# Hybrid layer on one core: which engine builds the S5 stage's block-diagonal pieces, diagonal terms and weight splits

## Chip, core and metric

The kernel runs on one core of a Trainium2 chip. TensorE does the matrix products, VectorE, ScalarE and GpSimd the elementwise work, and SyncE's queue issues nearly all transfers. In the rows they are PE (and PEld for its weight loads), DVE, ACT, POOL and SP. The metric is the device time of one execution in microseconds (us), lower is better; a comparison goes by the median of several runs.

## The reference, cut to what matters

One decoder layer on 1024 tokens of width 1024: RMSNorm, one combined projection, three branches (an S5 diagonal complex state-space model, a Mamba-2 SSD, cross-attention into 256 memory tokens), a gated merge, an output projection, then a gated convolutional MLP and a last norm. All data are float32. The part around the change is the S5 branch:

```python
bbr = fr[..., None] * b_re - fi[..., None] * b_im
bbi = fr[..., None] * b_im + fi[..., None] * b_re
bu_re = jnp.einsum('blgk,gpk->blgp', ug, bbr)
bu_im = jnp.einsum('blgk,gpk->blgp', ug, bbi)
...
_, _, xr, xi = lax.associative_scan(combine, (a_re, a_im, bu_re, bu_im), axis=1)
y = jnp.einsum('gkp,blgp->blgk', c_re, xr) - jnp.einsum('gkp,blgp->blgk', c_im, xi)
return y.reshape(bsz, L, D_S5) + d * u
```

There are 64 groups of 16 channels with 64 states each.

## The kernel before, in words

Each float32 product is made of three matmuls on halves: a weight tile `wr` comes from memory, ScalarE rounds it into `wh`, and the low part `wl = wr - wh` is a subtraction on a second engine (`split_into`, L140). `w_ent` (L260) makes these splits for the jobs to come; the set `on_pool` (L226) names the jobs whose subtraction is on GpSimd instead of VectorE. A ring of six `wh`/`wl` pairs runs ahead of TensorE, and three `wr` tiles ahead of that: the next load of a `wr` tile waits in SyncE's queue, which is served in order, until the last reader of the old one, the subtraction, is done.

The stage of the change lies about 523 to 780 us into the span. TensorE projects the four query tiles (`qt`) and nine gate tiles (`gt`), in half tiles called `gh`, with 24 matmuls each; after every 12 of them a step of the S5 work (`s5_work`, L773) may be put in, paced by `RATE_S5` and `S5_LAG`. S5 runs in four rounds (q = 0 to 3, 16 groups each), and a round goes like this:

- `b_maps` (L825): six VectorE operations make the tiles `s5BAr`, `s5BAi`; eight columns of them are copied (the imaginary part negated) into the block-diagonal tile `s5bd`, in four pieces of 64 partitions x 128 elements.
- `phases` and `double` (L888, L896): GpSimd builds the rotation tiles `s5Rr`, `s5Ri` in seven doublings, 42 small operations, from 8 up to 512 elements per partition; `s5ph` is their scratch.
- `b_transpose` and `c_maps`: TensorE transposes (`s5bps`, `s5cps`), ScalarE copies, and VectorE makes the maps `s5CAr`, `s5CAi` in six operations of 1024 elements, the last two of them with both inputs in SBUF.
- `lag_maps` (L865): TensorE multiplies `s5CAr`, `s5CAi` with `s5bd` (16 pairs of matmuls, `s5kps`); ScalarE copies the result to a tile (`s5w` in the rows), a diagonal term `s5dg` is made and added to it, and the tile goes over memory (`kS`) into the tile `s5T`.
- `sums`, `scan`, `back`: TensorE makes `s5sr`, `s5si`; VectorE rotates them with `s5Rr`, `s5Ri`, scans, and rotates back into `s5Hr`, `s5Hi`, in two halves.
- `outputs` and `gelu`: TensorE makes `s5yp` of the round before; ScalarE and VectorE make `s5Y`, which is stored (`yS`) from a single buffer.

While this stage is written down, TensorE, ScalarE and SyncE keep the order of the program (`TE.on = SY.on = S.on`, L1151); VectorE's and GpSimd's order is set by a scheduler. Each engine then runs its own list strictly in order, and waits at the head of it. All operations go through one recording helper, so every row says L51; rows are told apart by tile names.

Of the kernel before, what the change touches and what calls it, by code (L numbers as in the profile page):

```python
# [12 lines left out]
ALU = mybir.AluOpType  # L13
# [4 lines left out]
P = 128  # L18
# [8 lines left out]
C_U, C_Z, C_X, C_DT, C_Q, C_G = 0, 1024, 3072, 6144, 6176, 6688  # L27
# [31 lines left out]
def hybrid_layer(ctx: ExitStack, tc: tile.TileContext, a: dict, out: bass.AP):  # L59
    nc = tc.nc  # L60
    V, S, G, TE, SY = (InOrder(tc, e) for e in (nc.vector, nc.scalar, nc.gpsimd, nc.tensor, nc.sync))
# [63 lines left out]
    def tt(o, i0, i1, op, e=V):  # L125
        e.tensor_tensor(out=o, in0=i0, in1=i1, op=op)

    def ts(o, i0, s1, op0, s2=None, op1=None, e=V):
        if s2 is None:
            e.tensor_scalar(out=o, in0=i0, scalar1=s1, scalar2=None, op0=op0)  # L130
        else:
            e.tensor_scalar(out=o, in0=i0, scalar1=s1, scalar2=s2, op0=op0, op1=op1)
# [4 lines left out]
    def copy(o, i, scale=1.0):  # L137
        S.activation(out=o, in_=i, func=AF.Copy, scale=scale)
# [9 lines left out]
    def bc(ap, n):  # L148
        return ap.unsqueeze(len(ap.shape)).to_broadcast(list(ap.shape) + [n])
# [41 lines left out]
    G_S5, G_ATT, G_SSD = range(0, 9), range(9, 12), range(12, 24)  # L191

    def win(c0, m=P):
        return ("p", "w_in", 0, KD, c0, m)
# [28 lines left out]
    T_AT = {n: i for i, n in enumerate(("T1", "T2", "T3", "T4"))}  # L223
    dents = [(p, k) for p in PRODS for k in range(NK)]

    on_pool = {win(C_U), win(C_U + P)} | {win(C_Q + m * P) for m in range(4)} | {win(C_G + m * P) for m in G_S5}  # L226
    raw_list, ents = [], []
    for n, jb in enumerate(jobs):
        if jb[0] == "w":
# [543 lines left out]
    def s5_work():  # L773

        with ExitStack() as es:
# [4 lines left out]
            bd = sp.tile([P, 2, NCH, 2, 16], F32, name="s5bd")  # L780
# [8 lines left out]
            def wt():  # L789
                return sp.tile([P, 8, P], F32, tag="w", name="s5w", bufs=2)  # L790

            def fl(t, s0, n):
                return t.rearrange("p j s k -> p j (s k)")[:, :, s0 * 16:(s0 + n) * 16]
# [17 lines left out]
            def cmap(o, s0, wr, wi, p2, jj):  # L811

                shp = [P, 8, 8, 16]
                orr, oi = (t[:, :, s0:s0 + 8, :] for t in o)
                w = [x.unsqueeze(2).to_broadcast(shp) for x in (wr, wi)]
                p_ = [bc(x[:, jj, :], 16) for x in p2]
                t1, t2 = (wt().rearrange("p j (t k) -> p j t k", t=8) for _ in range(2))
                tt(orr, w[0], p_[0], ALU.mult)
                tt(t1, w[1], p_[1], ALU.mult)
                tt(oi, w[0], p_[1], ALU.mult)  # L820
                tt(t2, w[1], p_[0], ALU.mult)
                tt(orr, orr, t1, ALU.subtract)
                tt(oi, oi, t2, ALU.add)

            def b_maps(jj, braw):  # L825

                BAr = sp.tile([P, 8, 8, 16], F32, tag="BAr", name="s5BAr")
                BAi = sp.tile([P, 8, 8, 16], F32, tag="BAi", name="s5BAi")
                cmap((BAr, BAi), 0, braw[:, 0], braw[:, 1], (pfr, pfi), jj)
                for g2 in range(2):  # L830
                    pp = slice(g2 * 64, (g2 + 1) * 64)
                    G.tensor_copy(bd[pp, 0, :, g2, :], BAr[pp, :, 7, :])
                    G.tensor_scalar(out=bd[pp, 1, :, g2, :], in0=BAi[pp, :, 7, :], scalar1=-1.0,
                                    scalar2=0.0, op0=ALU.mult, op1=ALU.add)
                return BAr, BAi

            def c_transpose(craw):
# [27 lines left out]
            def lag_maps(q, CA):  # L865

                ksq = kS[q % 2]
                ktw = wt()
                for hh in range(2):
                    kps = ps.tile([32, 4, P], F32, tag="s", name="s5kps")  # L870
                    for j in range(4):
                        jx = hh * 4 + j
                        for ri in range(2):
                            TE.matmul(kps[:, j, :], bd[:, ri, jx].rearrange("p g k -> p (g k)"),
                                      fl(CA[ri], 0, 8)[:, jx, :], start=ri == 0, stop=ri == 1)
                    KT = ktw[0:32, 4 * hh:4 * hh + 4, :]
                    copy(KT, kps)
                    dg = sp.tile([32, 4, 16], F32, tag="dg", name="s5dg")
                    tt(dg, bc(dk[:, 8 * q + 4 * hh:8 * q + 4 * hh + 4], 16),
                       id16.unsqueeze(1).to_broadcast([32, 4, 16]), ALU.mult, G)  # L880
                    tt(KT[:, :, 0:16], KT[:, :, 0:16], dg, ALU.add, G)
                    SY.dma_start(out=ksq[4 * hh:4 * hh + 4].rearrange("j p x -> p j x"), in_=KT)
                kv_ = ksq.rearrange("j (g k) x -> k j g x", g=2)
                for s in range(8):
                    tz = Tz[s * 16:(s + 1) * 16].rearrange("p (j g) t k -> p j g (t k)", g=2)
                    SY.dma_start(out=tz[:, :, :, s * 16:P], in_=kv_[:, :, :, 0:P - s * 16])
# [114 lines left out]
            for q in range(5):  # L1001
# [4 lines left out]
                if q < 4:  # L1006
                    U, braw, craw = nl
                    BA = b_maps(jj, braw)
                    R = phases(jj)
                    double(R, jj, range(5))  # L1010
# [16 lines left out]
                if q == 4:  # L1027
                    s5_end.append(lambda: y_store(qo, 1, Y1))
                    break
                lag_maps(q, CA)  # L1030
                if old:
                    y_store(qo, 1, Y1)
# [16 lines left out]
    id16 = cp.tile([32, 16], F32, name="id16")  # L1049
# [814 lines left out]
```

## Time and profile before

| what | us |
|---|---|
| median of 3 runs | 2323.52 (2322.17 to 2324.78) |
| profiled execution | 2324.85 |
| its span, first to last instruction | 2323.1 |
| TensorE matmul busy | 2210.0 (95%) |
| VectorE busy | 1649.3 (71%) |
| ScalarE busy | 981.4 (42%) |
| GpSimd busy | 857.6 (37%) |
| TensorE busy in 543 to 563, 614 to 625, 672 to 683, 735 to 755 | 6.15 of 20, 5.73 of 11, 6.40 of 11, 15.32 of 20 |

TensorE is the engine whose list is never far from being the limit, so the places where it stands still are what counts. The page's slices show a 3 to 6 tenths busier GpSimd and a less busy TensorE in the 9th to 12th of 40 slices, which is the S5 stage. The table's last line holds the four stretches of that stage where TensorE does little.

### The profile page before, as it was taken

Reading aid. Unit: us, or ns where it says so; the run is one execution under the profiler, and the core shown is the slowest. Engines: PE = TensorE matmul, PEld = TensorE weight load, DVE = VectorE, ACT = ScalarE, POOL = GpSimd, SP = SyncE. Lnnn points to the kernel's source line nnn. Section 1 sums busy time; section 2 is a strip of 40 time slices with the busy share of each in tenths; the row PEclk is TensorE's granted clock in tenths of the full one; section 3 lists DMA queues with packets and bytes.
Section 4 is the critical chain, followed back from the end, with each engine's and each line's share of the span. In section 5 each row is a group of like instructions: output and inputs, shape, how many; then the busy total and the mean of one; then the engine's idle time right before and its main releaser. Section 6 shows DMA issues by size and latency. Waiting matters only on the chain. (4 is left out here: it accounts for less than half of the span.)

```text
span 2323.1 us, 31155 instructions
## 1 busy us (share of the span) xinstructions
PE 2210.0 (95%) x11239; PEld 1828.8 (79%) x11239; DVE 1649.3 (71%) x2310; ACT 981.4 (42%) x1746; POOL 857.6 (37%) x689
## 2 busy tenths in 40 slices
PE   6989999997898999999989999999999999999997
PEld 5777888886777788777768878889878888888886
DVE  7899878876664685989564455642888888886665
ACT  4444554552222266566342121222345545545543
POOL 4423333337666003888337522220123343320111
PEclk9999999998999999999999999999999999999999
DMA  4323434455353446898777764523323323229654
GB/s 149 110 82 91 127 109 127 127 139 96 92 107 82 128 139 231 272 315 268 232 258 240 226 207 145 163 73 119 109 68 96 118 86 118 86 102 330 223 186 152
DMA packets 380474, 356.06 MB, mean 153 GB/s; under 512 B 35616, under 2 KB 323232, under 8 KB 380320
## 3 DMA queue, kind: packets, MB, share of 16 engines
q1 hardware_dynamic: 379168, 349.89, 48.5%
q10 hardware_dynamic: 1152, 4.19, 0.4%
q8 instruction: 88, 1.44, 0.3%
q14 instruction: 66, 0.54, 0.1%
HBM read 255.97 MB, written 98.04 MB: 152 GB/s over the span
## 5 line engine op out<-in xcount | busy, mean ns | idle before, releaser
L51 DVE TENSOR_TENSOR wl<-wr,wh 128x512 fp32r<-128x512 f32 (+1 forms) x275 | 233.4, 859 | 168.6 <-ACT wh L51 167.0
L51 ACT ACTIVATE wh<-wr 128x512 fp32r<-128x512 f32 (+1 forms) x305 | 185.9, 625 | 326.7 <-PE g L51 149.1
L51 PE MATMUL g<-hlH,wh 128*128 128x512 f32 x736 | 288.6, 394 | 11.3 <-ACT hlH L51 5.7
L51 PE MATMUL g<-hlL,wh 128*128 128x512 f32 x736 | 290.1, 394 | 4.6 <-DVE hlL L51 4.5
L51 PE MATMUL g<-hlH,wl 128*128 128x512 f32 x736 | 288.1, 392 | 0.0
L51 POOL TENSOR_TENSOR wS<-wr 128x512 f32<-128x512 f32 x82 | 132.0, 1610 | 374.4 <-DMA wr<-in_w_up 181.9
L51 PE MATMUL gh<-hlH,wh 128*128 128x512 f32 (+1 forms) x464 | 191.9, 414 | 0.0
L51 PE MATMUL gh<-hlH,wl 128*128 128x512 f32 (+1 forms) x464 | 181.6, 391 | 0.0
L51 PE MATMUL gh<-hlL,wh 128*128 128x512 f32 (+1 forms) x464 | 181.5, 391 | 0.0
L51 PEld LDWEIGHTS g<-hlH,wh 128*128 128x128 f32 x736 | 139.2, 189 | 42.4 <-issue 6.8
L51 PEld LDWEIGHTS g<-hlL,wh 128*128 128x128 f32 x736 | 139.0, 189 | 37.9 <-DVE hlL L51 9.9
L51 ACT ACTIVATE wh<-wS 128x512 fp32r<-128x512 f32 x164 | 102.2, 628 | 145.0 <-PE wA L51 89.1
L51 PEld LDWEIGHTS g<-hlH,wl 128*128 128x128 f32 x736 | 139.2, 189 | 28.4
L51 DVE TENSOR_TENSOR wl<-wS,wh 128x512 fp32r<-128x512 f32 x164 | 135.5, 831 | 36.6 <-ACT wh L51 36.4
L51 POOL TENSOR_TENSOR wS<-wr,wS 128x512 f32<-128x512 f32 x41 | 95.1, 2318 | 109.0 <-DVE wl L51 99.1
L51 PE MATMUL dP<-wl,ah 128*128 128x512 f32 x308 | 120.0, 390 | 0.2 <-DVE wl L51 0.2
L51 PE MATMUL dP<-wh,ah 128*128 128x512 f32 x308 | 119.9, 389 | 0.1
L51 PE MATMUL dP<-wh,al 128*128 128x512 f32 x308 | 119.8, 389 | 0.0
L51 POOL TENSOR_TENSOR x1f<-x1f,gfin 128x512 f32<-128x512 f32 x16 | 23.0, 1459 | 224.3 <-ACT sq L51 224.3
L51 PEld LDWEIGHTS gh<-hlH,wh 128*128 128x128 f32 (+1 forms) x464 | 86.2, 186 | 24.1 <-issue 5.7
L51 DVE TENSOR_TENSOR al<-ra,ah 128x512 fp32r<-128x512 f32 x77 | 56.3, 731 | 66.9 <-ACT ah L51 66.8
L51 PEld LDWEIGHTS gh<-hlL,wh 128*128 128x128 f32 (+1 forms) x464 | 86.3, 186 | 21.6 <-issue 3.6
(383 smaller groups left out, 6004.4 us busy)
## 6 DMA issues: line engine op xcount, KB each, us to landing
wr<-in_w_in SPq DMA_DIRECT2D x76, 512.0 KB, 3.7
wr<-in_w_up SPq DMA_DIRECT2D x44, 512.0 KB, 3.7
xc<-xcS SPq DMA_DIRECT2D x32, 640.0 KB, 5.8
ra<-aS SPq DMA_DIRECT2D x77, 256.0 KB, 5.2
seg<-aD SPq DMA_DIRECT2D x32, 512.0 KB, 6.5
gi<-gS SPq DMA_DIRECT2D x32, 512.0 KB, 5.4
xcS<-xv SPq DMA_DIRECT2D x24, 512.0 KB
gS<-gt SPq DMA_DIRECT2D x24, 512.0 KB, 3.0
```

The costliest lines, as they stand in the source:

```text
L51: r = f(*args, **kw)
```

## The change

Three sets of elementwise operations go from GpSimd to VectorE; the arithmetic is the same.

```diff
-    on_pool = {win(C_U), win(C_U + P)} | {win(C_Q + m * P) for m in range(4)} | {win(C_G + m * P) for m in G_S5}
+    on_pool = {win(C_U), win(C_U + P)}
...
-                    G.tensor_copy(bd[pp, 0, :, g2, :], BAr[pp, :, 7, :])
-                    G.tensor_scalar(out=bd[pp, 1, :, g2, :], in0=BAi[pp, :, 7, :], scalar1=-1.0,
-                                    scalar2=0.0, op0=ALU.mult, op1=ALU.add)
+                    V.tensor_copy(bd[pp, 0, :, g2, :], BAr[pp, :, 7, :])
+                    ts(bd[pp, 1, :, g2, :], BAi[pp, :, 7, :], -1.0, ALU.mult)
...
                     tt(dg, bc(dk[:, 8 * q + 4 * hh:8 * q + 4 * hh + 4], 16),
-                       id16.unsqueeze(1).to_broadcast([32, 4, 16]), ALU.mult, G)
-                    tt(KT[:, :, 0:16], KT[:, :, 0:16], dg, ALU.add, G)
+                       id16.unsqueeze(1).to_broadcast([32, 4, 16]), ALU.mult)
+                    tt(KT[:, :, 0:16], KT[:, :, 0:16], dg, ALU.add)
```

The first line concerns 13 jobs of two entries, so 26 subtractions `wl`; the second 16 pieces of `s5bd`; the third 8 terms `s5dg` and 8 additions. The lists of TensorE, ScalarE and SyncE are the same as before. GpSimd's and VectorE's lists change.

GpSimd at the end of the first round, before: the last operation of the phases, then all that followed it.

```order
L51 TENSOR_TENSOR s5Ri<-s5Ri,s5ph 128x8x64
L51 TENSOR_TENSOR wl<-wr,wh 128x512
L51 COPY s5bd<-s5BAr 64x8x16 x2
L51 TENSOR_SCALAR s5bd<-s5BAi 64x8x16 x2
L51 TENSOR_TENSOR wl<-wr,wh 128x512 x2
L51 TENSOR_TENSOR s5w<-s5w,s5dg 32x4x16
L51 TENSOR_TENSOR s5dg<-s5dk,id_389 32x64
L51 TENSOR_TENSOR s5w<-s5w,s5dg 32x4x16
L51 TENSOR_TENSOR s5dg<-s5dk,id_389 32x64
L51 MEMSET s5D_4769 128x8
```

In the changed list the phases are followed by a memset of the decay tile and at once by the phases of the next round; the pieces of `s5bd`, which stood behind all 42 operations, are gone from the list.

VectorE in the second round, a piece of the difference: the end of `b_maps`, then the operations of `gelu` and the first of `c_maps`.

```order
 L51 TENSOR_TENSOR s5BAr<-s5BAr,s5w 128x1024
 L51 TENSOR_TENSOR s5BAi<-s5BAi,s5w 128x1024
+L51 COPY s5bd<-s5BAr 64x8x16
+L51 TENSOR_SCALAR s5bd<-s5BAi 64x8x16
+L51 COPY s5bd<-s5BAr 64x8x16
+L51 TENSOR_SCALAR s5bd<-s5BAi 64x8x16
+L51 TENSOR_TENSOR wl<-wr,wh 128x512 x2
 L51 SCALAR_TENSOR_TENSOR s5Y<-s5Y,s5yp 128x4x128 x4
 L51 TENSOR_TENSOR s5CAr<-s5cps,s5pwr 128x8x128
```

The four pieces of `s5bd` now come right behind the maps that they are copied from, ahead of `gelu` and of `c_maps`, and a pair of `wl` with them.

VectorE later in the same round, between the two halves of `scan` and `back`: another pair of `wl` stands between the second scan and the second `back`.

```order
 L51 TENSOR_TENSOR s5w<-s5w 128x512 x2
 L51 SCALAR_TENSOR_TENSOR s5W<-s5D_5271,s5w 128x512 x2
+L51 TENSOR_TENSOR wl<-wr,wh 128x512 x2
 L51 TENSOR_TENSOR s5Hr<-s5W,s5Rr 128x4x127
 L51 TENSOR_TENSOR s5w<-s5W,s5Ri 128x4x127
```

`back` now has to wait for these subtractions, and they for ScalarE's `wh`. In the first round the pair stands between the first scan and the first `back`.

## Rows read from the trace of the kernel before

**Rows 1.** Who waited for whom, 500 to 770 us: total us, times, longest.

```profile
POOL wl L51 <- ACT wh L51: 63.8, 7, 19.5
...
PE s5kps L51 <- POOL s5bd L51: 31.0, 7, 13.7
DVE s5CAr L51 <- ACT s5CAi L51: 30.8, 4, 10.2
...
ACT s5Y L51 <- DMA yS<-s5Y: 19.3, 2, 16.5
```

**Rows 2.** TensorE in order of time: start, us, operation [idle before, released by].

```profile
556.92 0.63 PE L51 MATMUL s5kps<-s5CAr,s5bd 128*32 128x128 f32 x2 [13.75 <-POOL s5bd L51]
557.66 0.64 PE L51 MATMUL s5kps<-s5CAi,s5bd 128*32 128x128 f32 x2
...
562.27 0.38 PE L51 MATMUL s5kps<-s5CAr,s5bd 128*32 128x128 f32 x2
562.49 0.38 PE L51 MATMUL s5kps<-s5CAi,s5bd 128*32 128x128 f32 x2
...
619.90 0.64 PE L51 MATMUL s5kps<-s5CAi,s5bd 128*32 128x128 f32 x2 [2.46 <-POOL s5bd L51]
...
677.24 0.63 PE L51 MATMUL s5kps<-s5CAi,s5bd 128*32 128x128 f32 x2 [1.35 <-POOL s5bd L51]
...
736.04 0.64 PE L51 MATMUL s5kps<-s5CAi,s5bd 128*32 128x128 f32 x2 [2.43 <-POOL s5bd L51]
...
740.74 1.09 PE L51 MATMUL s5sr<-s5U,s5BTr 128*64 128x128 f32 x16
...
746.34 1.97 PE L51 MATMUL s5sr<-s5U,s5BTr 128*64 128x128 f32 x16 [3.63 <-DVE s5Y L51]
```

**Rows 3.** Busy time in a stretch: PE, PEld, DVE, ACT, POOL, granted clock, DMA.

```profile
543.00:563.00 20.00, 6.15 (x34) 4.71 (x34) 3.33 (x3) 0.68 (x2) 17.08 (x21) 0.66 0.26 73
```

**Rows 4.** SyncE's queue, its longest wait: total us, times, longest.

```profile
SPq L51 <- POOL s5D L51: 25.6, 1, 25.6
```

**Rows 5.** SyncE's queue in order of time: the store behind that wait.

```profile
737.82 3.92 SPq L51 DMA_DIRECT2D yS<-s5Y  x8
```

**Rows 6.** VectorE in order of time: the last map of each round.

```profile
544.70 1.63 DVE L51 TENSOR_TENSOR s5CAi<-s5CAi,s5w 128x1024 f32<-128x1024 f32 x1
...
613.98 2.28 DVE L51 TENSOR_TENSOR s5CAi<-s5CAi,s5w 128x1024 f32<-128x1024 f32 x1
...
672.64 2.06 DVE L51 TENSOR_TENSOR s5CAi<-s5CAi,s5w 128x1024 f32<-128x1024 f32 x1
...
732.92 1.31 DVE L51 TENSOR_TENSOR s5CAi<-s5CAi,s5w 128x1024 f32<-128x1024 f32 x1
```

**Rows 7.** Groups by shape, 500 to 770 us: count | busy us, mean ns | idle before.

```profile
L51 POOL TENSOR_TENSOR wl<-wr,wh 128x512 fp32r<-128x512 f32 x26 | 37.0, 1438 | 67.3 <-ACT wh L51 63.8 <-issue 1.9 <-POOL s5bd L51 0.8
```

**Rows 8.** Groups by shape, VectorE: one split in this stretch, and small scalings.

```profile
L51 DVE TENSOR_TENSOR wl<-wr,wh 128x512 fp32r<-128x512 f32 x1 | 0.7, 686 | 0.0
...
L51 DVE TENSOR_SCALAR dgi<-ident,ivt 128x128 f32<-128x128 f32 x8 | 1.9, 280 | 0.0
```

**Rows 9.** First round in order of time: a scan, ScalarE's splits, the last back, outputs.

```profile
570.81 2.33 DVE L51 TENSOR_TENSOR_SCAN s5W<-s5D,s5w 128x512 f32<-128x512 f32 x2
...
572.93 1.14 ACT L51 ACTIVATE wh<-wr 128x512 fp32r<-128x512 f32 x2
...
578.23 0.68 DVE L51 SCALAR_TENSOR_TENSOR s5Hi<-s5Hi,s5w 128x508 f32<-128x508 f32 x1
...
583.12 0.60 PE L51 MATMUL s5yp<-s5U,s5T 128*128 128x128 f32 x4
```

**Rows 10.** Second round in order of time: GpSimd's phases, first and last, TensorE's sums.

```profile
586.79 8.42 POOL L51 TENSOR_TENSOR s5ph<-s5keep,s5Ri 128x8 f32<-128x8 f32 x1
...
617.95 1.27 POOL L51 TENSOR_TENSOR s5Ri<-s5Ri,s5ph 128x512 f32<-128x512 f32 x1
...
624.65 1.09 PE L51 MATMUL s5sr<-s5U,s5BTr 128*64 128x128 f32 x16
```

## The prediction, made before the changed kernel ran

> **What bounds the kernel now.** I read the share of busy time first (TensorE 95%), then, for the S5 stage, the waits by engine, TensorE's own list in order of time, SyncE's queue, and last VectorE's list at each place where TensorE stands still. The waits of the stage [rows 1] are long on nearly every engine, and most cost nothing: GpSimd is idle 63.8 us for ScalarE's `wh`, VectorE 30.8 us for ScalarE's copies. The line to pick out is the one whose waiting engine is TensorE: `s5kps` waits 31.0 us in seven waits for GpSimd's `s5bd`, the longest 13.7. TensorE's list shows where: at 556.92, and in the other rounds just ahead of the rows at 619.90, 677.24 and 736.04 [rows 2]. These are the pieces that the GpSimd list of the section on the change puts behind all phases. The stretch around the first wait has TensorE busy 6.15 of 20 us and GpSimd 17.08 [rows 3]: one engine stands for the other.
>
> A smaller stall is TensorE's 3.63 us at 746.34, named after VectorE's `s5Y` [rows 2]. Followed back it is a chain of buffers: SyncE's queue stands 25.6 us [rows 4] behind a load whose `wr` GpSimd has not read yet, the store `yS` comes out only at 737.82 and takes 3.92 [rows 5], ScalarE waits 16.5 us for it before it may write the single `s5Y` again [rows 1], VectorE waits for ScalarE and TensorE for VectorE. Behind the stall the same 16 matmuls take 1.97 instead of 1.09 us [rows 2].
>
> So in this stage TensorE loses 31.0 + 3.6 us in plain sight, and some more to the clock: the granted clock is 0.66 in that first stretch [rows 3], the lower level of 1.2 GHz for part of it. The 16 pairs of `s5kps` start over 5.57 us (556.92 to 562.49); at the distance of the last two, 0.22, fifteen gaps would take 3.3, so 2.3 us go there [rows 2].
>
> **The change, part by part.** The sum is made against the profiled execution, 2324.85 (span 2323.1 and 1.75 around it), which lies 1.33 above the median of 2323.52. The gain is then taken off the median.
>
> *Pieces of `s5bd`.* On VectorE they stand right behind `b_maps`, ahead of `c_maps`. So they are done before `s5CAr` and `s5CAi`, the other operands of the same matmuls, and `s5CAi` becomes the last one. Its last operation ends at 544.70 + 1.63 = 546.33, 613.98 + 2.28 = 616.26, 672.64 + 2.06 = 674.70 and 732.92 + 1.31 = 734.23 [rows 6]. In the first round one more `wl` ahead of the maps makes it 546.33 + 0.69 = 547.0. Against the starts of the second half of the operands in rows 2 (the first matmul with `s5CAi`) this is a gain of 557.66 - 547.0 = 10.6, 619.90 - 616.26 = 3.6, 677.24 - 674.70 = 2.5 and 736.04 - 734.23 = 1.8: together 18.5 of the 31.0. The remaining 12.5, about 3 a round, stay as a wait for VectorE.
>
> *What VectorE pays for it.* The 26 subtractions cost GpSimd 1438 ns each, 37.0 us in all [rows 7]. VectorE does one of the same shape in 686 ns, so 17.8 us come to it; and a small scaling of 128 x 128 took 280 ns [rows 8], which I take for each of the pieces (64 x 128) and as an upper end for the diagonal terms: 32 operations, at most 9 us. Per round that is four pieces, 1.1, a pair of `wl` ahead of `c_maps`, 1.4, and another pair by the scans. Ahead of `c_maps` VectorE waits for ScalarE 30.8 us in four waits [rows 1], the copies of TensorE's transposes; that wait hides 2.5 us except where it is itself shorter, and without this cover the round would gain 2.5 less (four rounds: 10). The diagonal terms lie behind `s5kps`, where VectorE waits for TensorE's sums, and cost nothing.
>
> *The pair by the scans.* It waits for `wh`, and everything behind it on VectorE's list (`back`, then `s5Hr`, `s5Hi` for TensorE's outputs) waits too. In the first round the first scans end at 570.81 + 2.33 = 573.14 and `wh` is there at 572.93 + 1.14 = 574.07: with the second subtraction 574.07 + 0.69 = 574.76, a delay of 1.6. The last operation of `back` ends at 578.23 + 0.68 = 578.91, the outputs start at 583.12: 4.2 us of slack [rows 9] cover it. If that cover were gone, it would cost 1.6 a round.
>
> *GpSimd.* In the second round its phases end at 617.95 + 1.27 = 619.2, with splits and pieces in between; the sums, whose rotation is the first reader, start at 624.65 [rows 10]. It has some 5 us of slack and loses work, so nothing new is late there.
>
> *A lock between the two engines.* At 586.79 an operation on 8 elements took GpSimd 8.42 us, where one on 512 elements took 1.27 [rows 10]; VectorE was in `b_maps` at the time. So a long VectorE stretch can hold a GpSimd operation up, and the subtractions add to such stretches. The price here lies between nothing, since the phases have about 5 us in hand, and 2.5 a round when it is VectorE's last two maps that wait for a GpSimd operation of 1.27 each. I take nothing: the maps ran beside the phases before as well, and their stretched times (2.28 and 2.06 against 1.31) are in my sum.
>
> The Trainium skill speaks against the change at this place ("SBUF — State Buffer", section "Who interferes with whom"): a VectorE instruction with two inputs in SBUF contends with a GpSimd instruction that reads SBUF, and whichever issues second is blocked until the other is done. `wl` has two such inputs. The 8.42 us agree with it. By that rule at its worst the time is that of the second rival below; by the rows' slack it changes nothing.
>
> *The store chain.* Without `wl` on GpSimd SyncE's queue does not stand behind the phases; `yS` leaves earlier, `s5Y` is free, and the stall of 3.63 goes. The sixteen matmuls behind it, twice (`s5sr` and `s5si`), run at 1.09 instead of 1.97: 1.8 more. Together 5.4; the bound below is nothing, if VectorE's `wl` hold the queue as long.
>
> Sum: 18.5 + 5.4 = 23.9. 2324.85 - 23.9 = 2300.95 for an execution like the profiled one, 2299.6 against the median.
>
> **Rivals.**
> - *More is gained.* If the shorter stalls no longer bring the clock down, up to 2.3 us a round come back; I take 2.3 for the first and half for each other, 5.8. If the last maps also run unstretched, at 1.31 each [rows 6] (1.0 + 0.75 + 0.3 = 2.0 for `s5CAi`, as much for its sister `s5CAr`), 4.0 more: 2299.6 - 9.8 = 2289.8. Against it: stalls of 2.46 and 1.35 were enough for matmuls of 0.63 to 0.64 in the rows [rows 2].
> - *The lock takes part of it.* Each of the last two maps waits for one GpSimd operation more, 2 x 1.27 = 2.5 a round, 10.2 in four: 2309.8. The same time comes out if ScalarE's copies don't cover the added 2.5. For it: 8.42 [rows 10]; against it: GpSimd has less to do.
> - *Slower: VectorE waits where GpSimd waited.* GpSimd was idle 63.8 us for `wh`, 44.3 without the longest wait [rows 1], some 11.1 a round. If these waits fall to VectorE ahead of `back`, each round pays 11.1 less the 4.2 of slack [rows 9], 27.6 in all, and 4 x 1.4 for the subtractions: 2299.6 + 33.2 = 2332.8. It decides once the delay passes 4.2 + 23.9 / 4 = 10.2 a round. Against it: in the first round ScalarE's `wh` come 0.9 after the scans [rows 9], not 11 us.
> - *It does not do what it says.* The stalls move to a later place where TensorE waits for a transfer or for VectorE: 2323.5.
>
> **How the numbers follow.** Forecast 2299.6, chance 0.53; its own range is 2294 (the clock comes back) to 2305 (the store chain stays, +5.4). More gained 0.17, the lock 0.20, slower 0.05, nothing 0.05. The range takes the first three and 2 us around the outer ones: 2288 to 2312. A measurement of this kernel tells about 0.2%, 4.6 us, from no change: faster 0.90, same 0.05, slower 0.05.
>
> **What would show it.** Right: TensorE's `s5kps` waits some 3 us a round for VectorE's `s5CAi` and no more for `s5bd`; SyncE's queue has no wait of 25 us for GpSimd; ScalarE's wait of 16.5 for `yS` and TensorE's of 3.63 at `s5sr` are gone; GpSimd ends its phases before the sums. Wrong: a wait for `wh` on VectorE of more than 4 us, outputs that wait for `s5Hr`, an `s5CAi` that ends later than the ends worked out above (less what was gained before), or sums that wait for `s5Rr`.

## The result, and the profile after

The changed kernel takes 2299.34 us (median of 4, 2295.98 to 2305.17) against 2324.15 for the kernel before on the same chip: ratio 0.9896, 95% interval 0.9881 to 0.9910, 24.8 us less. Beside two later groups of experiments it came to 0.9896 (0.9877 to 0.9915) and 0.9892 (0.9876 to 0.9909). The profiled execution took 2295.98, its span is 2294.3.

The waits of the stage in the changed kernel, 500 to 770 us (total us, times, longest), answer to [rows 1]:

```profile
POOL s5Ri L51 <- DVE s5Hi L51: 71.7, 3, 26.8
...
DVE s5CAr L51 <- ACT s5CAi L51: 17.9, 4, 7.0
...
PE s5kps L51 <- DVE s5CAi L51: 6.2, 4, 1.8
PE s5kps L51 <- DVE s5CAr L51: 5.2, 3, 1.9
```

TensorE's 31.0 us for `s5bd` are gone, and 11.4 us for VectorE's maps have come in their place (12.9 in both later profiles of the changed kernel). GpSimd now has its long waits for VectorE's `back` ahead of the phases, which cost nothing. Of ScalarE's 19.3 us for `yS` 0.9 are left.

TensorE in order of time in the changed kernel, the rows that answer to [rows 2]:

```profile
546.69 0.38 PE L51 MATMUL s5kps<-s5CAi,s5bd 128*32 128x128 f32 x2 [1.18 <-DVE s5CAi L51]
...
549.75 0.38 PE L51 MATMUL s5kps<-s5CAi,s5bd 128*32 128x128 f32 x2
...
602.77 0.60 PE L51 MATMUL s5kps<-s5CAi,s5bd 128*32 128x128 f32 x2 [1.60 <-DVE s5CAi L51]
...
657.68 0.60 PE L51 MATMUL s5kps<-s5CAi,s5bd 128*32 128x128 f32 x2 [1.60 <-DVE s5CAi L51]
...
715.78 0.61 PE L51 MATMUL s5kps<-s5CAi,s5bd 128*32 128x128 f32 x2 [1.82 <-DVE s5CAi L51]
...
722.41 1.04 PE L51 MATMUL s5sr<-s5U,s5BTr 128*64 128x128 f32 x16
...
753.33 0.39 PE L51 MATMUL s5yp<-s5Hi,s5CAi 64*128 64x128 f32 x4
```

The last row is TensorE's last S5 work of the stage. In the kernel before it was here:

```profile
780.31 0.39 PE L51 MATMUL s5yp<-s5Hi,s5CAi 64*128 64x128 f32 x4
```

So 26.98 of the 28.8 us between the two spans are won inside the stage. Each round's wait is now short and names `s5CAi`; the second sums start at 722.41 with no wait, where [rows 2] had 3.63. From there to the end of the stage the granted clock is at the upper level, where it was 0.91 before; first the kernel before, then the changed one:

```profile
746.30:780.70 34.40, 34.35 (x213) 28.11 (x213) 24.47 (x38) 10.18 (x19) 3.48 (x6) 0.91 0.45 114
...
722.40:753.70 31.30, 31.30 (x217) 25.86 (x213) 23.02 (x38) 6.13 (x12) 0.11 (x1) 1.00 0.45 108
```

The same stretch as in [rows 3], in the changed kernel (PE, PEld, DVE, ACT, POOL, granted clock, DMA):

```profile
543.00:563.00 20.00, 18.82 (x146) 15.71 (x145) 18.48 (x21) 4.23 (x7) 11.49 (x11) 1.00 0.45 73
```

TensorE is busy 18.82 us there instead of 6.15, at the upper level of its clock. SyncE's queue, which stood 25.6 us in one piece [rows 4], issues the store of [rows 5] at 701.93, and none of its waits names GpSimd any more:

```profile
701.93 3.64 SPq L51 DMA_DIRECT2D yS<-s5Y  x8
```

VectorE's last maps answer to [rows 6]:

```profile
544.91 1.63 DVE L51 TENSOR_TENSOR s5CAi<-s5CAi,s5w 128x1024 f32<-128x1024 f32 x1
...
600.57 2.06 DVE L51 TENSOR_TENSOR s5CAi<-s5CAi,s5w 128x1024 f32<-128x1024 f32 x1
...
655.47 2.06 DVE L51 TENSOR_TENSOR s5CAi<-s5CAi,s5w 128x1024 f32<-128x1024 f32 x1
...
713.35 2.28 DVE L51 TENSOR_TENSOR s5CAi<-s5CAi,s5w 128x1024 f32<-128x1024 f32 x1
```

The fourth, 1.31 us before, now takes 2.28. GpSimd's phases of the second round answer to [rows 10]:

```profile
573.65 8.51 POOL L51 TENSOR_TENSOR s5ph<-s5keep,s5Ri 128x8 f32<-128x8 f32 x1
...
601.62 2.13 POOL L51 TENSOR_TENSOR s5Ri<-s5Ri,s5ph 128x512 f32<-128x512 f32 x1
```

They end at 603.75, ahead of the sums of that round. What VectorE pays for the moved work is listed by shape, 500 to 770 us (count | busy us, mean ns):

```profile
L51 DVE TENSOR_TENSOR wl<-wr,wh 128x512 fp32r<-128x512 f32 x31 | 21.8, 732 | 13.8 <-ACT wh L51 13.7
L51 DVE TENSOR_TENSOR s5w<-s5w,s5dg 32x64 f32<-32x64 f32 x8 | 3.5, 432 | 0.4
L51 DVE TENSOR_TENSOR s5dg<-s5dk,id 32x64 f32<-32x64 f32 x8 | 3.3, 418 | 0.1
L51 DVE COPY s5bd<-s5BAr 64x128 f32<-64x128 f32 x8 | 2.0, 248 | 0.1
L51 DVE TENSOR_SCALAR s5bd<-s5BAi 64x128 f32<-64x128 f32 x8 | 2.0, 244 | 0.0
```

The pieces cost 4.0 us and the diagonal terms 6.8, together 10.8 (at most 9 were foreseen). Over the whole span VectorE is busy 26.2 us more than before, 1675.5 instead of 1649.3; at most 26.8 were foreseen.

### The profile page after: what moved, and what is told of

Read it like the earlier page. It is cut to its first block, busy times and chain, and to the rows that moved or that the text cites. A ratio compares the mean times of both kernels' runs of the same rounds, so it can differ in the third digit from the quotient of the medians.

```text
span 2294.3 us, 31144 instructions
## 1 busy us (share of the span) xinstructions
PE 2206.8 (96%) x11239; PEld 1827.4 (80%) x11239; DVE 1675.5 (73%) x2368; ACT 980.7 (43%) x1746; POOL 819.2 (36%) x631
## 5 line engine op out<-in xcount | busy, mean ns | idle before, releaser
L51 DVE TENSOR_TENSOR wl<-wr,wh 128x512 fp32r<-128x512 f32 x301 | 255.1, 859 | 176.1 <-ACT wh L51 169.6
```

The lines of the kernel that those rows point to most:

```text
L51: r = f(*args, **kw)
```

## The experiments

Ratios are to the kernel before in the same group of runs, with the 95% interval.

**The pieces alone.**

```diff
-                    G.tensor_copy(bd[pp, 0, :, g2, :], BAr[pp, :, 7, :])
-                    G.tensor_scalar(out=bd[pp, 1, :, g2, :], in0=BAi[pp, :, 7, :], scalar1=-1.0,
-                                    scalar2=0.0, op0=ALU.mult, op1=ALU.add)
+                    V.tensor_copy(bd[pp, 0, :, g2, :], BAr[pp, :, 7, :])
+                    ts(bd[pp, 1, :, g2, :], BAi[pp, :, 7, :], -1.0, ALU.mult)
```

> Only the 16 pieces of s5bd go to VectorE; the 26 subtractions and the diagonal terms stay on GpSimd. My theory (the stall is the place of the pieces behind the phases): s5kps waits for VectorE's s5CAi instead, the gain is the 18.5 us of the four rounds plus some 2 us of clock in the first, so about 2304 us against 2324, ratio 0.991; the store chain of 5.4 stays in the fourth round. Rival (the subtractions on GpSimd are what made it late): less than 9 us of gain, 2315 or more.

Measured: 2315.61 us, 0.9963 (0.9948 to 0.9978), 9.5 us less than before by the medians. The time fits the rival, the mechanism does not. The waits for `s5bd` are gone, but the store chain has grown. In order of time in this run: TensorE, GpSimd, SyncE's queue, ScalarE, TensorE.

```profile
721.56 1.09 PE L51 MATMUL s5sr<-s5U,s5BTr 128*64 128x128 f32 x16
...
723.61 2.48 POOL L51 TENSOR_TENSOR wl<-wr,wh 128x512 fp32r<-128x512 f32 x2
...
726.12 0.38 SPq L51 DMA_DIRECT2D wr<-in_w_in  x1
726.59 3.89 SPq L51 DMA_DIRECT2D yS<-s5Y  x8
...
732.32 0.60 ACT L51 ACTIVATE s5Y<-s5yp 128x512 f32<-128x512 f32 x1 [21.96 <-DMA yS<-s5Y]
...
735.08 1.97 PE L51 MATMUL s5sr<-s5U,s5BTr 128*64 128x128 f32 x16 [11.55 <-DVE s5Y L51]
```

This is one chain: GpSimd does the subtraction only behind the phases, SyncE's load of `wr` waits for it, the store `yS` stands behind that load, ScalarE may not write `s5Y` for 21.96 us, and TensorE waits 11.55 us instead of 3.63 and then runs its sums in 1.97. TensorE starts the first sums at 721.56, 19.18 us ahead of [rows 2] (740.74), about the gain that was expected; behind the obstacle it is 11.26 ahead (735.08 against 746.34). It had come earlier to the same chain, and the longer wait there took the difference.

**The pieces, and one pair of subtractions out of 13.** The pieces as in the run above, and this line:

```diff
-    ... | {win(C_G + m * P) for m in G_S5}
+    ... | {win(C_G + m * P) for m in G_S5 if m != 7}
```

> The run that moves the pieces alone, and one of the 13 pairs of subtractions with them: the pair that the load of wr at 726.12 waits for in that run (GpSimd did it at 723.61, behind the phases of the fourth round). My theory (this pair holds SyncE's queue, behind it the store yS, and through the single s5Y TensorE's sums): the wait of 11.55 us at s5sr goes, and the half clock behind it, 12 to 14 us off the run with the pieces alone (2315.6), about 2302, ratio 0.990; the other 12 pairs carry next to nothing. Rival (the subtractions matter by their number, as load on GpSimd): less than 3 us off, 2313 or more.

Measured: 2302.80 us, 0.9910 (0.9891 to 0.9929). The load goes out 19 us earlier, and the store with it, in SyncE's queue of this run:

```profile
706.77 0.38 SPq L51 DMA_DIRECT2D wr<-in_w_in  x1
710.74 3.64 SPq L51 DMA_DIRECT2D yS<-s5Y  x8
```

TensorE has no wait at `s5sr` any more. So two subtractions of 26 hold 12.8 us between these two runs. The other 24 hardly count: with all 26 moved and the diagonal terms left on GpSimd, in the runs further down, the ratio is 0.9916 and 0.9914.

**The subtractions alone.**

```diff
-    on_pool = {win(C_U), win(C_U + P)} | {win(C_Q + m * P) for m in range(4)} | {win(C_G + m * P) for m in G_S5}
+    on_pool = {win(C_U), win(C_U + P)}
```

> Only the 26 subtractions go to VectorE; the pieces of s5bd stay on GpSimd behind all phases. My theory: the pieces come earlier by the one or two subtractions of 1.3 to 1.4 us that stood ahead of them, 1.4 in the first round and at most 2.6, 2.5 and 1.8 in the others (8.3), and the store chain of the fourth round goes (5.4): 13.7 us, about 2310, ratio 0.994; the 13.7 us wait of the first round is still there, a little shorter. Rival (the subtractions carry the gain): over 18 us. Rival (VectorE waits for ScalarE's halves instead): no gain, 2324.

Measured: 2320.85 us, 0.9979 (0.9965 to 0.9992), 4.3 us less, about what the store chain alone is worth. The 8.3 us that the pieces should have come earlier did not stay: TensorE's last pair of `s5kps` starts 0.6, 1.4 and 0.8 us earlier than before in the first three rounds and 1.8 later in the fourth (742.22 against 740.43). The second round in this run, GpSimd and VectorE in order of time:

```profile
585.71 9.63 POOL L51 TENSOR_TENSOR s5ph<-s5keep,s5Ri 128x8 f32<-128x8 f32 x1
...
593.98 1.29 DVE L51 TENSOR_TENSOR wl<-wr,wh 128x512 fp32r<-128x512 f32 x2
595.18 0.68 DVE L51 SCALAR_TENSOR_TENSOR s5Y<-s5Y,s5yp 128x512 f32<-128x512 f32 x1
...
614.08 2.13 POOL L51 TENSOR_TENSOR s5Ri<-s5Ri,s5ph 128x512 f32<-128x512 f32 x1
616.15 0.64 POOL L51 COPY s5bd<-s5BAr 64x128 f32<-64x128 f32 x2
```

The copies of this round in the kernel before:

```profile
615.12 1.63 POOL L51 COPY s5bd<-s5BAr 64x128 f32<-64x128 f32 x2
```

GpSimd's first small operation is held from 585.71 to 595.34, until VectorE's moved pair has ended at 595.27: 9.63 us instead of the 8.42 of [rows 10]. The last one takes 2.13 instead of 1.27, beside VectorE's maps. Even so the phases of this round end 3.0 us earlier than in [rows 10] (616.21 against 619.22), and the pieces have nothing of it, because their place has changed: in the list before the two copies stood ahead of the last two operations of the phases, here they stand behind them. In the fourth round the phases themselves end 3.6 us later than before, at 735.25. So the lock is real, but here it holds GpSimd's phases, where the prediction's second rival had it hold VectorE's maps; how much of the lost 8.3 us is this hold and how much the new place in the list was not tried apart.

**The pieces on GpSimd, ahead of the phases.** The first operation of the phases is ordered behind the last piece.

```diff
-                    G.tensor_scalar(out=bd[pp, 1, :, g2, :], ...)
+                    bd_last[0] = G.tensor_scalar(out=bd[pp, 1, :, g2, :], ...)
...
+                for m_ in (G.memset(Rr[:, :, 0:1], 1.0), G.memset(Ri[:, :, 0:1], 0.0)):
+                    tc.add_manual_dep(m_.ins, bd_last[0].ins.name, ..., reason="order")
```

> The kernel before, all operations on their engines, but on GpSimd's list the pieces of s5bd are put ahead of the phases of the same round. My theory (the place in the list counts, not the engine): the wait for s5bd goes as when the pieces are on VectorE, within 3 us of the run that moves them alone, about 2304 to 2307. Rival (the phases, which now start only behind b_maps, come late for the rotation of the sums): a new wait of VectorE for s5Rr or s5Ri, less than half of that gain, 2314 or more.

Measured: 2309.63 us, 0.9929 (0.9907 to 0.9951), 6 us under the move of the pieces to VectorE alone, where at most 3 were expected between the two. Of the waits at `s5kps` none names `s5bd`, and they come to 11.7 us against 11.8 there: for this wait the place in the list decides and not the engine. The lower time comes from the store chain. The pair of subtractions of the fourth round stays on GpSimd too, but in this run it stands ahead of the phases, and the store goes out behind it; GpSimd, then SyncE's queue:

```profile
710.91 1.30 POOL L51 TENSOR_TENSOR wl<-wr,wh 128x512 fp32r<-128x512 f32 x1
...
712.71 3.90 SPq L51 DMA_DIRECT2D yS<-s5Y  x8
```

TensorE has no wait at `s5sr` here: it starts the first sums of that round 5.6 us later than with the pieces alone (727.16 against 721.56) and the second ones 6.1 earlier (728.96 against 735.08). So for the subtractions as well it is the place behind the phases that costs. The run stays behind the whole change, in part by the rival that was named: the phases of the first round start only behind `b_maps`. VectorE and TensorE in this run:

```profile
560.05 0.69 DVE L51 TENSOR_TENSOR s5w<-s5sr,s5Rr 128x512 f32<-128x512 f32 x1 [14.15 <-POOL s5Rr L51]
...
573.67 0.49 PE L51 MATMUL s5yp<-s5Hr,s5CAr 64*128 64x128 f32 x4 [1.33 <-DVE s5Hr L51]
```

VectorE waits 14.15 us for `s5Rr`, and the outputs wait for `s5Hr`.

**The change without the diagonal terms,** twice, the second time beside the whole change. The edit is the first two parts of the change.

> The change without its third part: pieces and subtractions on VectorE, the diagonal terms stay on GpSimd. My theory: the diagonal terms lie behind s5kps and carry nothing, so the time is that of the changed kernel, 2299 within 3 us, ratio 0.989 to before. Rival (the terms on GpSimd hold up the tile that goes over memory): 5 us slower or more than the change, 2304 or above, and outputs that wait for s5T.

> The change without its third part (diagonal terms on GpSimd) once more, beside the whole change on one chip and in more rounds, since the first comparison left 0.2% open. My theory (the terms lie behind s5kps and cost TensorE nothing by themselves): within 2 us of the run of the whole change beside it. Rival (they are worth the 4 to 6 us that the medians so far showed): 4 us or more above it.

> The whole change, as the base for the run beside it: 2299 to 2301 us, ratio to before 0.990.

Measured: 2305.03 us, 0.9916 (0.9898 to 0.9933), then 2302.99, 0.9914 (0.9902 to 0.9927); the whole change beside it 2300.52, 0.9892 (0.9876 to 0.9909). The medians differ by 2.5 us and the intervals overlap, so the times alone leave "within 2 us" open. The rows point the same way in both profiles: TensorE's last S5 work of the stage is at 756.42 and 756.68, 3 us later than in the three profiles of the whole change (753.33, 753.21, 753.42). VectorE and GpSimd in the first profile, order of time:

```profile
555.30 0.31 POOL L51 TENSOR_TENSOR s5w<-s5w,s5dg 32x64 f32<-32x64 f32 x1
...
558.13 0.69 DVE L51 TENSOR_TENSOR s5w<-s5si,s5Ri 128x512 f32<-128x512 f32 x1 [2.65 <-DMA kS<-s5w]
...
599.98 1.97 DVE L51 TENSOR_TENSOR s5CAr<-s5CAr,s5w 128x1024 f32<-128x1024 f32 x1
601.87 2.28 DVE L51 TENSOR_TENSOR s5CAi<-s5CAi,s5w 128x1024 f32<-128x1024 f32 x1
```

The addition stands behind the phases, the store `kS` behind it, and VectorE waits 2.65 us for the buffer. In the next round the maps then take 1.97 and 2.28 us (1.25 and 2.06 in the whole change). That the later scan is what moves GpSimd's phases further into the maps fits the order of the rows; it was not tried apart.

**Each moved subtraction twice.**

```diff
+    s5_jobs = {win(C_Q + m * P) for m in range(4)} | {win(C_G + m * P) for m in G_S5}
...
+        if jobs[n] in s5_jobs:
+            tt(l, src, h.bitcast(F32), ALU.subtract)
```

> The changed kernel, where VectorE makes each of the 26 moved subtractions twice, 17.9 us more of work on it at 686 ns each. My theory (VectorE's waits for ScalarE, 17.9 us in four ahead of c_maps, and the slack of back cover such work): 0 to 4 us above the change, 2300 to 2304, the first round's maps later by one subtraction. Rival (VectorE is at its limit in this stage, or holds GpSimd's phases up long enough to delay the scans): 10 us or more above, 2310, with TensorE waiting for s5Hr or VectorE for s5Rr.

Measured: 2301.13 us, 0.9901 (0.9886 to 0.9916): no difference from the change that can be measured, with 26 more subtractions and 18.9 us more on VectorE (busy 1694.4 us, 1675.5 in the change). Its waits ahead of `c_maps` shrink, in the waits of this run (17.9 in the change):

```profile
DVE s5CAr L51 <- ACT s5CAi L51: 10.3, 4, 4.5
```

**GpSimd kept out of the last map.** A copy of one column from `s5CAi` into `s5Rr`, overwritten at once, makes GpSimd wait.

```diff
-                    double(R, jj, [6])
                     CA = c_maps(jj, cps)
+                    G.tensor_copy(R[0][:, 0, 64:65], CA[1][:, 0, 8, 15:16])
+                    double(R, jj, [6])
```

> The changed kernel, where GpSimd's last doubling waits (from its third operation on) until VectorE has made s5CAi, so that VectorE's last map runs beside an idle GpSimd. My theory (the two block each other when both read two tiles from SBUF): the last map takes 1.2 us in each round instead of 1.63 to 2.28, TensorE's second wait in s5kps is shorter by 0.4, 0.8, 0.8 and 1.1, some 3 us in all and up to as much again by the clock; the time is 3 to 5 us under the change, 2294 to 2296. Rival (the map is long for another reason): the map keeps its 2 us and the time is that of the change or, by later phases, above it.

Measured: 2298.08 us, 0.9882 (0.9864 to 0.9900); the change beside it, expected and measured:

> The changed kernel as it is, as the base for the runs beside it: 2299 us as before, within 4 us, ratio 0.990.

2301.29 us, 0.9896 (0.9877 to 0.9915). The times don't tell them apart, the rows do. VectorE and GpSimd in the second and third round of this run:

```profile
597.73 1.04 POOL L51 TENSOR_TENSOR s5Ri<-s5keep,s5Ri 128x512 f32<-128x512 f32 x1
...
601.81 1.22 DVE L51 TENSOR_TENSOR s5CAi<-s5CAi,s5w 128x1024 f32<-128x1024 f32 x1
...
603.09 0.18 POOL L51 COPY s5Rr<-s5CAi 128x1 f32<-128x1 f32 x1 [4.32 <-DVE s5CAi L51]
...
654.77 2.02 POOL L51 TENSOR_TENSOR s5Ri<-s5keep,s5Ri 128x512 f32<-128x512 f32 x1
...
655.82 2.06 DVE L51 TENSOR_TENSOR s5CAi<-s5CAi,s5w 128x1024 f32<-128x1024 f32 x1
```

With GpSimd idle the map takes 1.22 us. In the third round one of GpSimd's operations still ran beside it, and both are long, 2.02 and 2.06 (alone 1.04 and 1.22). The expectation held for the second and fourth round only.

**The maps one step earlier,** on the changed kernel and on the kernel before. `c_maps`, here divided into its two copies and its six operations (`c_rest`), is written right behind the transposition of C, ahead of `b_transpose`; TensorE's list stays the same, on ScalarE's the two copies of C come ahead of the four of B.

```diff
-                cmap((CAr, CAi), 1, cps[:, 0], cps[:, 1], (pwr, pwi), jj)
                 return CAr, CAi
+
+            def c_rest(jj, cps, CA):
+
+                cmap(CA, 1, cps[:, 0], cps[:, 1], (pwr, pwi), jj)
...
                     cps = c_transpose(craw)
+                    CA = c_maps(jj, cps)
+                    c_rest(jj, cps, CA)
                     double(R, jj, [5])
...
                     double(R, jj, [6])
-                    CA = c_maps(jj, cps)
```

> The changed kernel, with c_maps written one step earlier: ScalarE copies the transposed C ahead of the copies of the transposed B, so VectorE need not wait for those. My theory (what is left of the stall is VectorE waiting for ScalarE's list, not VectorE's load): TensorE's waits in s5kps, 11.4 us in seven places, go, and with them the lower clock behind them (8 pairs of matmuls a round at 0.43 instead of 0.22 us in three rounds, 1.5 to 1.7 each): 14 to 16 us under the change, 2283 to 2286, ratio to before 0.983. Rival (VectorE is full, the maps move and gelu or the subtractions come later instead): under 5 us of gain, with new waits for s5Y or wl.

> The kernel before, with c_maps one step earlier as in the run that did this to the changed kernel (there it gave some 16 us). My theory (here GpSimd's pieces of s5bd are the operand that comes last, so an earlier s5CAi gives nothing of its own): the waits of s5kps for s5bd stay, 28 us or more of the 31, and the time is 2320 to 2325, ratio 0.998 to 1.000; the little that may be gained is GpSimd's large phases running beside fewer two-input maps, about 1 us a round. Rival (the two gains are independent): ratio 0.993 or less, 2310.

Measured on the changed kernel: 2284.34 us, 0.9822 (0.9805 to 0.9839), 17 us under the change beside it; better than both kernels. Of the seven waits at `s5kps` only 0.37 and 1.18 in the first round are left. VectorE and TensorE in the second round of this run, and the busy times and the clock there:

```profile
585.64 1.22 DVE L51 TENSOR_TENSOR s5CAr<-s5cps,s5pwr 128x1024 f32<-128x1024 f32 x1
...
591.41 1.64 DVE L51 TENSOR_TENSOR s5CAi<-s5CAi,s5w 128x1024 f32<-128x1024 f32 x1
...
596.42 0.41 PE L51 MATMUL s5kps<-s5CAr,s5bd 128*32 128x128 f32 x2
```

```profile
595.00:610.00 15.00, 15.00 (x131) 13.04 (x130) 12.34 (x17) 5.29 (x10) 7.48 (x8) 1.00 0.59 122
```

VectorE starts the maps at once, without the wait of up to 7.0 us for ScalarE, and they end at 593.05, ahead of TensorE's `s5kps` at 596.42; TensorE is busy throughout, at the upper clock.

On the kernel before the same edit gives 2325.59 us, 1.0002 (0.9990 to 1.0015), nothing. Its waits:

```profile
PE s5kps L51 <- POOL s5bd L51: 31.3, 7, 13.6
```

The 31 us for `s5bd` are untouched, as expected (the time is 0.6 us above the range that was given): there the pieces were the operand that came last.

## Why the prediction was right

The forecast was 2299.6 us, within 0.3 of the median. By the rows of TensorE its terms came out as follows; each line is the shift between [rows 2] and the rows above, less the shift already there.

| step | forecast | measured |
|---|---|---|
| first round, 557.66 to 546.69 | 10.6 | 10.97 |
| its matmuls, by the clock: last pair 562.49 to 549.75 | 0 | 1.77 |
| second round, 619.90 to 602.77 | 3.6 | 4.39 |
| third round, 677.24 to 657.68 | 2.5 | 2.43 |
| fourth round, 736.04 to 715.78 | 1.8 | 0.70 |
| wait at `s5sr`, 746.34 to 722.41 | 3.6 | 3.67 |
| clock behind it, to the end of the stage, 780.31 to 753.33 | 1.8 | 3.05 |
| behind the stage, to the span | 0 | 1.8 |
| sum | 23.9 | 28.8 |

The sum of the profiled execution is 4.9 above the forecast, but that execution is the fastest of the four; by the medians it is 24.8.

That the median came within 0.3 us is in part luck. Inside the stage the change gains more than the forecast: TensorE's last S5 work is 26.9 to 27.1 us earlier in all three profiles, 3 us above the 23.9. Behind the stage the three executions take 1.8 us less, 2.7 more and 1.3 more than the one before. The cause of this scatter stays open; by the medians 24.8 of the 27 us are left. Without the third part of the change, which the forecast put at nothing, the stage ends 23.9 and 23.6 us earlier: the two parts that the sum holds come to the sum (17.4 by the fourth round instead of 18.5, and 1.2 more by the clock at the end), and the diagonal terms are the 3 us above it.

- **Pieces of `s5bd`.** Right in place and size, 18.5 in both columns (10.97 + 4.39 + 2.43 + 0.70 = 18.49), and right that 12.5 us stay as a wait for VectorE's maps (11.4). The ends of the maps were the right bound in three rounds. In the fourth the map went from 1.31 to 2.28 us: the lock, which I had priced at nothing beyond the times already in the rows; it cost 1.0 there, while the second round gained 0.8. The prediction has the pieces behind all phases; this is so in the first and fourth round, while in the second and third the copies stood ahead of the last one or two operations of the phases and only the scalings behind all. The sum does not hang on this, since it starts from TensorE's rows.
- **The clock.** In the profiled execution the first round's matmuls ran at 0.22 us a pair; in another profile of the same kernel they ran at the lower level behind waits of 1.62 and 1.18, and in the third at 0.22 again behind 1.60 and 1.18. This term is no fixed part of the gain; the first two lines of the table together come to 12.7, 12.9 and 13.2 in these three. The prediction's remark that stalls of 2.46 and 1.35 were enough for the lower level left out the waits of 4.86 and 4.37 that TensorE had 3 and 2 us ahead of them.
- **The store chain.** Right for the whole change (3.67 of 3.6), and the clock behind it gave 1.2 more than the two rows that I had counted (0.91 granted before, 1.00 after, to the end of the stage). What the sum didn't say is that this price holds only ahead of the other gain: with the pieces alone moved, it is 11.55 us and the matmuls behind it. The two parts are worth 9.5 and 4.3 us apart and 20 to 22 together. To add them was right for the whole, and wrong as a statement on either part.
- **What VectorE pays.** Right: another 18.9 us of the same work cost nothing that can be measured.
- **Diagonal terms.** I had them at nothing. Two profiles show 3 us; by the rows it is the store that waits behind the phases and the buffer that waits for the store. Nor was 280 ns an upper end for them: they took 418 and 432 on the mean.
- **Rivals.** The lock exists and costs 0.4 to 1.1 us a map (1.63 to 2.28 against 1.22 alone), not the 2.5 a round that would have made it 2309.8; in the run with the subtractions alone it also holds GpSimd's phases, and there the pieces stood behind them. Two of the signs named for being wrong did come, at little price. VectorE waits 5.46 us for `wh`, more than the 4 that were named, but at 762.58, behind the last `s5Hi` and TensorE's last S5 work; TensorE is busy 45.00 of 45 us from 755 to 800, and no output waited for `s5Hr`, so the slower rival did not happen. And `s5CAi` of the fourth round ends at 715.63, 1.0 later than 734.23 less the 19.56 gained before: the lock again.

## What to carry to other kernels

Where one engine's list holds the small pieces of a product behind a long run of other work, ask which operand comes last before and after the move: the gain ends at the next one, and an earlier `c_maps`, worth 17 us after the change, was worth nothing ahead of it. An in-order DMA queue ties a load that waits for one engine to every store behind it, so follow the queue as well as the engines; when TensorE comes earlier to such a chain, the same chain costs more. Parts of a change that lie on one path should be priced together and tried apart.

## What the runs showed of the hardware

- GpSimd's first operation of the phases with two inputs, on 8 elements, took 8.4 to 8.6 us beside VectorE's `b_maps`, and 9.63 when VectorE had one more pair of two-input subtractions behind them; in the run with the pieces ahead of the phases, where `b_maps` is over by then, it took 0.22. It came free when VectorE came to an instruction with at most one input in SBUF: `s5Y`, whose other input is in PSUM, at 595.18 in the run with the subtractions alone, and the copy of a piece at 581.88 in the changed kernel, where the hold ends at 582.16. The Trainium skill ("SBUF — State Buffer", section "Who interferes with whom") speaks of being blocked until the first instruction is done; with larger operations on both sides the rows agree with that (2.02 and 2.06 instead of 1.04 and 1.22), for the first operation of the phases the hold is longer than any one instruction. So the prediction's word that the 8.42 us agree with this rule is only half right: that there is a hold, not how long it lasts.
- In the run with the pieces alone, two instructions of 1.25 us on GpSimd, behind a long list there, cost TensorE a wait of 11.55 us by way of SyncE's queue, a buffer and two engines.
- The same waits of TensorE did not always bring its clock down: behind 1.55 and 0.76 us in the fourth round of the run with GpSimd kept out, 710 to 724 us, the granted clock stayed at 1.00, and behind the same two waits in its second round, 595 to 610 us, it was 0.89. What made the difference stays open.
